# Appending the sample's new keys to the second half of the cached keys in a planned two-thread transformer step

## The chip, the core and the metric

One core of one Trainium2 chip runs one step of a four-branch encoder in float32. The metric is the device time of one execution, in microseconds, as the median of several. Busy times, waits and orders are read from one profiled execution and from the built programs.

## The reference, cut to what matters

Each of two layers projects the input, runs three parallel branches (a gated MLP, latent attention "B", stick-breaking attention "C"), mixes them and runs an MLP. It does so for a prompt of 512 rows and for a sample of 8 streams with 16 new rows each. In the sample, both attentions look at 1024 cached keys and at the stream's own 16 new ones:

```
ckv_all = jnp.concatenate([ckv_p, ckv], 1)     # 1024 cached + 16 new, per stream
k_all = jnp.concatenate([k_p, kc], 1)
...
scores = (einsum('bqhc,bkc->bhqk', q_lat, ckv) + einsum('bqhr,bkr->bhqk', q_rope, krope)) * MLA_SCALE
p = softmax(where(visible, scores, -inf)); out = einsum('bhqk,bkc->bqhc', p, ckv)
...
z = einsum('bqhd,bkhd->bhqk', q, k) * SB_SCALE
log_skip = where(mask, log_sigmoid(-z), 0); suffix = reversed cumsum(log_skip) - log_skip
w = where(mask, exp(log_sigmoid(z) + suffix), 0); out = einsum('bhqk,bkhd->bqhd', w, v)
```

## The kernel before, in words

The program consists of two threads, P (the prompt) and S (the sample). Each thread is a generator that records its instructions through the wrappers `Timed` (line 399; every compute instruction has line 417) and `Loads` (line 425; every DMA has line 433). `weave` alternates the threads while recording. Then `Plan.schedule` (line 209) takes the recorded instructions with their dependences and a table of costs (`cost_of`, line 379) and writes the order of every engine by list scheduling: for each engine it takes the ready instruction with the lowest rank. `ranks` spreads thread S over a fixed part of each layer of thread P. A buffer of a tag (a ring of `bufs` tiles) is granted in program order and comes free when the last instruction on it is placed. `follow` pins the order that results. All loads go through the one queue of SP.

A float32 number is split into a rounded high part and the remainder, `hi` and `lo` (`split`, line 611: ACT writes the high part, DVE or POOL the low one). Products are made of these parts.

Thread S runs, per layer, `s_prep`, then `lane_smla` (branch B, line 1545), then `lane_ssb` (branch C, line 1621), then its output projection and MLP (`s_out_mlp`). During the two lanes thread P runs its own latent attention, output projection and MLP on the tag `acc` of PSUM; S uses the tags `sC` (3 banks) and `x` (2 banks).

Both lanes go through four pairs of streams (`pr` 0 to 3; a stream in the pair is `j`). `pipeline` (line 1525) runs three steps on each pair:

- `front` calls `sample_scores` (line 1438). For each stream and each half `c` of its cache (512 keys) and each 128 of the key's 256 elements (`ct`), it loads 128x512 keys (`rawK`), splits them into the tile `cT` (POOL makes the low part), and multiplies (`block`): 64 rows of high and 64 rows of low queries stand side by side as the 128 columns of the stationary operand, so each product has 128 output rows. Branch B adds one product with the rotary keys `kr`. `fold_to` (line 1420) adds the low rows to the high rows: an ACT copy of 64 rows into `tmp`, a DVE addition into the row tile (`s2` in branch B, shown as `s`; `z` in branch C). The products of a half are accumulated in a bank of `sC` in branch B and of `x` in branch C.
- The new keys are a block of their own, `fresh` (line 1458): the 128 new keys of all eight streams (`cnT`/`krN`, `knTs`) are multiplied with the stream's queries into another bank of `sC`, folded into columns 1024 to 1151 of the row, and all but the pair's own are masked out by a window of a 224-column mask (`msk`). So a row has 1152 columns.
- `mid` makes the weights over the 1152 columns: a softmax, or the stick-breaking passes with a scan (`stick_weights`, line 701).
- `back` transposes the row in nine pieces of 128 columns (`weights_T`, line 1426, tile `pTs`), multiplies the first eight with the cached values (`cN`) and the ninth, of 128 new positions, with all 128 new values (`cnh`, `vn`; `fresh` in `sample_values`, line 1499), and folds the result.

`rms_to` (line 659) writes the squares that it only sums into one tile `junk` that both threads share.

Of the kernel before, what the change touches and what calls it, by code (L numbers as in the profile page):

```python
# [96 lines left out]
class Plan:  # L97
# [111 lines left out]
    def schedule(self, prio):  # L209
# [24 lines left out]
        for p, t in tags:  # L234
# [51 lines left out]
        def issue(k, e, s):  # L286
# [212 lines left out]
def hybrid_step(  # L499
# [156 lines left out]

    junk = cp.tile([128, 512], BF16, name="junk")
# [767 lines left out]

    def weights_T(pl, p):
        pTs = pl.tile([128, 9, 2, 2, 64], F32R, tag="pTs", name="pTs")
        for c0 in range(0, 9, 4):
            n = min(4, 9 - c0)
            yield at("sC", p)  # L1430
            pt = bank("sC")
            for i in range(n):
                tr(pt[:, i * 128:(i + 1) * 128], p[:, (c0 + i) * 128:(c0 + i + 1) * 128])
            split(pTs[:, c0:c0 + n, :, 0], pTs[:, c0:c0 + n, :, 1],
                  pt[:, :n * 128].rearrange("p (i j c) -> p i j c", j=2, c=64))
        return pTs

    def sample_scores(pl, s2, src, q_of, new, msk, n, kr_of=None, kr_new=None):

# [4 lines left out]
        def run(f):  # L1444
            return at("none" if f.args[3] else acc, *(x for x in f.args[4:] if x is not None))

        def block(j, q, c, ct, c4, kr):
            if ct == 0:
                held.append(bank(acc))
            s_ = held[0]  # L1450
            pe.matmul(s_, q[ct], c4[:, 0], start=(ct == 0), stop=False)
            pe.matmul(s_, q[ct], c4[:, 1], start=False, stop=(ct == 1 and kr is None))
            if ct:
                if kr is not None:
                    pe.matmul(s_, q[2], kr, start=False, stop=True)
                fold_to(s2[64 * j:64 * j + 64, 512 * c:512 * c + 512], held.pop(), 512, pl)

        def fresh(j, q, s_):
            for ct in range(2):
                pe.matmul(s_[:, :128], q[ct], new[:, 0, ct], start=(ct == 0), stop=False)  # L1460
                pe.matmul(s_[:, :128], q[ct], new[:, 1, ct], start=False, stop=(ct == 1 and kr_new is None))
            if kr_new is not None:
                pe.matmul(s_[:, :128], q[2], kr_new, start=False, stop=True)
            fold_to(s2[64 * j:64 * j + 64, 1024:], s_, 128, pl)

        for j in range(2):
            q = q_of(j)
            for c in range(2):
                kr = None
                for ct in range(2):  # L1470
                    raw = half(pl, "K", n)
                    ld.dma_start(raw, src(j, c)[:, ct])
                    c4 = pl.tile([128, 2, 512], F32R, tag="cT", name="cT", bufs=2)
                    split(c4[:, 0], c4[:, 1], raw, KLO)
# [12 lines left out]
    def sample_values(pl, pTs, src, new, done, n):  # L1487

# [56 lines left out]
    def lane_smla(l, ql):  # L1545
# [3 lines left out]
        olT = smp.tile([128, 2, NB, 4, QS], F32, name="olT")  # L1549
        msk = smp.tile([128, 224], F32, name="mskm")  # L1550
        ld.dma_start(msk, c_wide[:, 0])
# [8 lines left out]
        def front(pr):  # L1560
            s2 = st[pr] = smp.tile([128, 1152], F32, tag="s2", name="s2", bufs=2)

            def kr_of(j, c):
                raw = smp.tile([128, 512], F32, tag="krs", name="krs")
                ld.dma_start(raw, t_kr[l, 2 * pr + j, c])
                kr = smp.tile([128, 512], F32R, tag="kr", name="kr", bufs=2)
                act.copy(kr, raw)
                sub(kr[64:128], raw[64:128], kr[64:128], pool)
                return kr
# [3 lines left out]

            yield from sample_scores(smp, s2, keys(pr), q_of, cnT, msk[:, 96 - 32 * pr:224 - 32 * pr], KV["smla"][0], kr_of, krN)

# [6 lines left out]
        def back(pr, used):  # L1582
            s2, r = st.pop(pr)
            pTs = yield from weights_T(smp, s2)
            used[0] += 1
# [9 lines left out]

            yield from sample_values(smp, pTs, values(pr), cnh, done, KV["smla"][1])

# [23 lines left out]
    def lane_ssb(l):  # L1621
        sp_cm = pool_of(f"ssb{l}", "right")
        sp = sp_cm.__enter__()
        msk = sp.tile([128, 224], F32, name="msks")
        ld.dma_start(msk, c_wide[:, 1])
# [32 lines left out]
        def front(pr):  # L1658
            z = st[pr] = sp.tile([128, 1152], F32, tag="z", name="z", bufs=3)
# [4 lines left out]
            yield from sample_scores(sp, z, keys(pr), q_of, knT, msk[:, 96 - 32 * pr:224 - 32 * pr], KV["ssb"][0])  # L1664

        def mid(pr):
            z = st[pr]
            a = sp.tile([128, 1152], F32, tag="a", name="a")
            stick_weights(z, z, a, [(0, 1152)])

        def back(pr, used):
            pTs = yield from weights_T(sp, st.pop(pr))
            used[0] += 1
# [11 lines left out]

            yield from sample_values(sp, pTs, values(pr), vn, done, KV["ssb"][1])

# [125 lines left out]
def _constants():  # L1813
# [17 lines left out]

    x = np.arange(224)
    same = x[None, :] // QS == 6 + p[:, None] // 64
    wide = np.zeros((128, 2, 224), np.float32)
    wide[:, 0] = np.where(same, 0, neg)
# [66 lines left out]
```

## Time and profile before

| | |
|---|---|
| median of 3 runs | 1744.52 us (1735.86 to 1745.47) |
| the profiled execution's own time | 1738.5 us |
| its span, first to last instruction | 1736.6 us |
| PE busy | 1665.9 us (96%), 8756 matmuls |
| PE weight loads busy | 1404.2 us (81%) |
| DVE, ACT, POOL busy | 1167.8, 1017.5, 461.8 us |
| mean granted TensorE clock | 0.988 |

The profile's page gives busy time by engine, the same in 40 slices, the chain of work that ended last, and groups of equal instructions. "PE" is matmuls, "PEld" their weight loads, which run beside earlier matmuls. The busy time of a group counts the tails of its matmuls, which overlap the next ones; how far apart matmuls follow each other is read from the start times in the timeline, or from a long stretch of the chain.

### The profile page before, as it was taken

The numbers are of one execution on the slowest core, as the hardware profiler recorded it, in microseconds if no ns is written. First come the engines' busy times: TensorE is split into PE (matmuls) and PEld (weight loads), VectorE is DVE, ScalarE is ACT, GpSimd is POOL, SyncE is SP. The second block draws the span as 40 slices with busy tenths as digits, with TensorE's granted clock in tenths as the row PEclk, the third lists the DMA queues.
The fourth block names the chain that finished last, engine by engine and source line by source line (L and its number), as shares of the span: only waits on it lengthen the run. The fifth ranks groups of instructions, "written<-read, shape, count | busy, mean of one in ns | idle before, by whom it ended". The sixth has DMA issues, their size and how long they took to land.

```text
span 1736.6 us, 24320 instructions
## 1 busy us (share of the span) xinstructions
PE 1665.9 (96%) x8756; PEld 1404.2 (81%) x8756; DVE 1167.8 (67%) x1592; ACT 1017.5 (59%) x1891; POOL 461.8 (27%) x320
## 2 busy tenths in 40 slices
PE   8999999899998999999999989999999999999998
PEld 6898988787886778888878988888778778788886
DVE  3487776846675587666744876868467766776766
ACT  4586785546664556463335857855467656564632
POOL 0000446534664300000000004466446552000000
PEclk9999999999999999999999999999999999999999
DMA  7236565445444587674353255665465456875732
GB/s 260 92 97 184 184 186 197 157 151 186 158 153 133 182 274 251 204 246 141 130 165 105 91 170 171 197 217 170 142 184 168 134 154 232 265 246 191 252 125 84
DMA packets 145817, 305.05 MB, mean 176 GB/s; under 512 B 32032, under 2 KB 46496, under 8 KB 145696
## 3 DMA queue, kind: packets, MB, share of 16 engines
q1 hardware_dynamic: 145696, 303.49, 54.2%
q8 instruction: 69, 1.13, 0.3%
q14 instruction: 52, 0.43, 0.1%
HBM read 286.14 MB, written 17.30 MB: 175 GB/s over the span
## 4 chain that ended last, share of the span: by engine, by line
PE 73%; ACT 8%; DVE 7%; DMA 7%; issue 4%; POOL 2%; SPq 0%; ACTq 0%; POOLq 0%; DVEq 0%
PE acc L417 52%; PE sC L417 11%; PE x L417 10%; DVE xy L417 2%; POOL cN L417 1%; DMA rawV<-in_t_ckvv_dram 1%; DMA rawK<-in_t_sbk_dram 1%; ACT w L417 1%; POOL cT L417 1%; DVE w L417 1%; ACT cN L417 1%; ACT cT L417 1%; DMA rawS<-in_w_up_dram 1%; DVE a L417 1%; DMA rawP<-in_w_down_dram 0%
## 5 line engine op out<-in xcount | busy, mean ns | idle before, releaser
L417 PE MATMUL acc<-yT,wx 128*128 128x512 f32 (+1 forms) x1632 | 398.2, 385 | 3.9 <-DVE yT L417 3.8
L417 PE MATMUL acc<-w,hT 128*128 128x512 f32 x1536 | 395.1, 398 | 2.3 <-DVE hT L417 1.7
L417 PEld LDWEIGHTS acc<-yT,wx 128*128 128x128 f32 x1632 | 291.8, 191 | 61.4 <-issue 3.9
L417 PEld LDWEIGHTS acc<-w,hT 128*128 128x128 f32 x1536 | 283.1, 189 | 65.5 <-DVE hT L417 2.1
L417 POOL TENSOR_TENSOR cT<-rawK,cT 128x512 fp32r<-128x512 f32 x128 | 200.8, 1575 | 164.2 <-ACT cT L417 120.3
L417 POOL TENSOR_TENSOR cN<-rawV,cN 128x512 fp32r<-128x512 f32 x128 | 195.1, 1532 | 168.6 <-ACT cN L417 164.5
L417 DVE TENSOR_TENSOR wS<-rawS,wS 128x1024 fp32r<-128x1024 f32 x144 | 175.0, 1223 | 82.9 <-ACT wS L417 82.7
L417 DVE TENSOR_TENSOR w<-rawP,w 128x1024 fp32r<-128x1024 f32 (+4 forms) x122 | 149.0, 1227 | 111.6 <-ACT w L417 110.0
L417 ACT CAST wS<-rawS 128x1024 fp32r<-128x1024 f32 x144 | 150.8, 1051 | 117.8 <-PE x L417 66.4
L417 PE MATMUL acc<-w,xT 128*128 128x512 f32 (+3 forms) x960 | 190.1, 353 | 2.2 <-ACT w L417 1.1
L417 PEld LDWEIGHTS acc<-w,xT 128*128 128x128 f32 x960 | 159.8, 193 | 20.5 <-ACT w L417 1.5
L417 ACT CAST w<-rawP 128x1024 fp32r<-128x1024 f32 (+4 forms) x122 | 122.5, 1006 | 73.3 <-DMA rawP<-in_w_down_dram 36.4
L417 DVE TENSOR_TENSOR xy<-xy,acc 128x512 f32<-128x512 f32 x128 | 86.6, 683 | 71.4 <-PE acc L417 70.8
L417 ACT CAST cN<-rawV 128x512 fp32r<-128x512 f32 x128 | 78.5, 620 | 66.0 <-DMA rawV<-in_t_sbv_dram 30.1
L417 PE MATMUL x<-cN,pTs 128*128 128x256 f32 x512 | 92.4, 290 | 11.5 <-ACT cN L417 5.8
L417 PEld LDWEIGHTS x<-cN,pTs 128*128 128x128 f32 x512 | 77.7, 190 | 30.3 <-ACT cN L417 11.8
L417 ACT CAST cT<-rawK 128x512 fp32r<-128x512 f32 x128 | 79.2, 620 | 36.4 <-PE sC L417 14.4
L417 PE MATMUL x<-wS,htS 128*128 128x512 f32 x384 | 99.5, 393 | 0.8 <-ACT htS L417 0.8
L417 PE MATMUL sC<-wS,x1TS 128*128 128x512 f32 x384 | 98.4, 394 | 0.0
L417 DVE TENSOR_TENSOR wx<-rawP,wx 128x1024 fp32r<-128x1024 f32 x68 | 85.9, 1265 | 12.6 <-ACT wx L417 11.9
L417 PEld LDWEIGHTS x<-wS,htS 128*128 128x128 f32 x384 | 72.0, 188 | 17.7 <-ACT htS L417 1.2
L417 PEld LDWEIGHTS sC<-wS,x1TS 128*128 128x128 f32 x384 | 71.8, 188 | 16.5 <-DVE wS L417 0.5
(277 smaller groups left out, 2635.2 us busy)
## 6 DMA issues: line engine op xcount, KB each, us to landing
rawP<-in_t_wup_dram SPq DMA_DIRECT2D x64, 512.0 KB, 4.0
rawP<-in_w_down_dram SPq DMA_DIRECT2D x64, 512.0 KB, 4.2
rawS<-in_w_up_dram SPq DMA_DIRECT2D x64, 512.0 KB, 4.6
rawS<-in_w_down_dram SPq DMA_DIRECT2D x64, 512.0 KB, 4.3
rawK<-in_t_ckv_dram SPq DMA_DIRECT2D x64, 256.0 KB, 3.0
rawV<-in_t_ckvv_dram SPq DMA_DIRECT2D x64, 256.0 KB, 3.1
rawK<-in_t_sbk_dram SPq DMA_DIRECT2D x64, 256.0 KB, 3.1
rawV<-in_t_sbv_dram SPq DMA_DIRECT2D x64, 256.0 KB, 3.0
```

What stands on the lines that cost most here:

```text
L417: r = f(out, *a, **k)
```

## The change

In `sample_scores` the tiles of the second half of the cache become 544 columns wide. Their last 32 columns take the pair's 32 new keys by a small ACT copy from `cnT`, `knTs` or `krN`. The products of that half are done in two parts of 272 columns into two banks (in branch C the second bank comes from `sC`), each folded by itself, and the separate block of 128 new keys is gone. A row is 1056 columns, the mask 32. In `weights_T` the ninth piece has 32 columns; its transposed weights are put on the 32 partitions where the pair's new values stand, and the values' `fresh` multiplies 32 partitions instead of 128. The planner gets a rule: the first instructions on a buffer wait until the first instruction on the buffer before it in the ring has been placed. `junk` becomes one tile for each thread.

```diff
@@ Plan.schedule
+        begun = [set() for _ in range(n)]
+        for p, t in tags:
+            for a, b in zip(t["names"], t["names"][1:]):
+                mine = self.tiles[b]["ops"]
+                for k in mine:
+                    if not ops[k]["deps"] & mine:
+                        begun[min(self.tiles[a]["ops"])].add(k)
+        for ks in begun:
+            for k in ks:
+                need[k] += 1
...
+            for x in begun[k]:
+                ready[x] = max(ready[x], s)
+                need[x] -= 1
+                if not need[x] and x not in glued:
+                    loose(x)
@@ rms_to
-        act.activation(junk[:, :n], src, AF.Square, accum_out=ss)
+        act.activation(junk[now["by"]][:, :n], src, AF.Square, accum_out=ss)
@@ weights_T
-        for c0 in range(0, 9, 4):
+        for c0 in range(0, 8, 4):
...
+        tr(pt[:32, :128], p[:, 1024:])
+        k = slice(32 * pr, 32 * pr + 32)
+        split(pTs[k, 8, :, 0], pTs[k, 8, :, 1], pt[:32, :128].rearrange("p (j c) -> p j c", j=2))
@@ sample_scores
         def block(j, q, c, ct, c4, kr):
+            n = 272 if c else 512
             if ct == 0:
-                held.append(bank(acc))
-            s_ = held[0]
-            pe.matmul(s_, q[ct], c4[:, 0], start=(ct == 0), stop=False)
-            pe.matmul(s_, q[ct], c4[:, 1], start=False, stop=(ct == 1 and kr is None))
+                held.extend([bank(acc)] + ([bank("sC")] if c else []))
+            for e in range(2):
+                for i, s_ in enumerate(held):
+                    pe.matmul(s_[:, :n], q[ct], c4[:, e, i * n:i * n + n], start=(ct == 0 and e == 0), stop=(ct == e == 1 and kr is None))
...
-        def fresh(j, q, s_):
...
-            yield at("sC")
-            fresh(j, q, bank("sC"))
...
+                    c4 = pl.tile([128, 2, 544], F32R, tag="cT", name="cT", bufs=2)
+                    split(c4[:, 0, :512], c4[:, 1, :512], raw, KLO)
+                    if c:
+                        act.copy(c4[:, :, 512:], new[:, :, ct, 32 * pr:32 * pr + 32])
...
+                        if c:
+                            act.copy(kr[:, 512:], kr_new[:, 32 * pr:32 * pr + 32])
@@ sample_values
-            pe.matmul(po[:, :256], w[8], new[:, 0], start=False, stop=False)
-            pe.matmul(po[:, :256], w[8], new[:, 1], start=False, stop=True)
+            k = slice(32 * pr, 32 * pr + 32)
+            pe.matmul(po[:, :256], w[8][k], new[k, 0], start=False, stop=False)
+            pe.matmul(po[:, :256], w[8][k], new[k, 1], start=False, stop=True)
```

The planner writes a new order for every engine. Three places of it follow. In the rows of the changed kernel the wrapper's line is 433.

TensorE in branch B of layer 0, second pair of streams, where a stream's new keys are multiplied (`cT`, `cnT`, `kr`, `krN` are keys, `qlT` and `qrS` queries, rows on `acc` are thread P's). Before:

```order
L417 MATMUL acc<-knT,qT 128x256 x3
L417 MATMUL acc<-krT,qrT 128x256 x2
L417 MATMUL sC<-cnT,qlT 128x128 x4
L417 MATMUL sC<-krN,qrS 128x128
L417 MATMUL acc<-mask,identr 128x128
L417 MATMUL acc<-knT,qT 128x256 x2
L417 MATMUL sC<-cT,qlT 128x512 x2
```

Now:

```order
L433 MATMUL acc<-knT,qT 128x256 x3
L433 MATMUL acc<-krT,qrT 128x256
L433 MATMUL sC<-cT,qlT 128x272 x8
L433 MATMUL sC<-kr,qrS 128x272
L433 MATMUL acc<-krT,qrT 128x256
L433 MATMUL acc<-mask,identr 128x128
L433 MATMUL acc<-ckT,w_2663 128x256 x3
L433 MATMUL sC<-kr,qrS 128x272
```

The five products of 128 columns are gone; the half that had five of 512 columns has ten of 272, and P's products stand between them as before.

TensorE at the end of the values of a pair in branch B of layer 0 (`cnh` are the new values, `identr,o` and `identr,s` transposes). Before:

```order
L417 MATMUL x<-cN,pTs 128x256 x3
L417 MATMUL x<-cnh,pTs 128x256 x2
L417 MATMUL acc<-w_5537,hT 128x512 x2
L417 MATMUL acc<-w_5589,hT 128x512 x3
L417 MATMUL acc<-w_5352,hT 128x512 x2
L417 MATMUL sC<-identr,o 128x128 x2
L417 MATMUL sC<-identr,s_3039 128x128 x8
```

Now:

```order
L433 MATMUL x<-cnh,pTs 128x256 x2
L433 MATMUL acc<-w_5635,hT 128x512 x2
L433 MATMUL acc<-w_5720,hT 128x512 x3
L433 MATMUL acc<-w_5470,hT 128x512 x2
L433 MATMUL sC<-identr,o 128x128 x2
L433 MATMUL sC<-identr,s_3082 128x128 x8
L433 MATMUL acc<-w_5470,hT 128x512
L433 MATMUL sC<-identr,s_3082 32x128
L433 MATMUL acc<-w_5537,hT 128x512 x3
```

The two products on `cnh`, which now use 32 partitions, and the ninth transpose, which now has 32 output rows, stand alone between full-size products of thread P.

ACT in branch B of layer 0, second pair (`rawK` to `cT` is the high part of the keys). Before:

```order
L417 COPY tmp<-sC 64x512
L417 CAST cqT<-acc 128x3x128
L417 CAST ckT<-acc 128x512
L417 CAST cT<-rawK 128x512 x2
L417 CAST kr<-krs 128x512
```

Now:

```order
L433 CAST cT<-rawK 128x512
L433 CAST cqT<-acc 128x3x128
L433 CAST ckT<-acc 128x512
L433 COPY cT<-cnT 128x2x32
L433 COPY tmp<-sC 64x512
L433 CAST cT<-rawK 128x512
L433 COPY cT<-cnT 128x2x32
L433 CAST kr<-krs 128x512
```

The copies of the new keys stand behind the casts of the same tile.

## Rows read from the trace of the kernel before

**Rows 1.** The page: busy time of each engine, and granted clock in 40 slices.

```profile
PE 1665.9 (96%) x8756; PEld 1404.2 (81%) x8756; DVE 1167.8 (67%) x1592; ACT 1017.5 (59%) x1891; POOL 461.8 (27%) x320
...
PEclk9999999999999999999999999999999999999999
```

**Rows 2.** Busy time by stage: stretch, length, engines (instructions), clock, DMA share, GB/s.

```profile
20.00:210.00 190.00, 184.49 (x1218) 169.76 (x1217) 121.73 (x232) 125.15 (x308) 23.99 (x22) 0.99 0.46 145
210.00:600.00 390.00, 368.97 (x1936) 307.24 (x1935) 255.72 (x342) 236.99 (x440) 204.73 (x132) 0.98 0.52 163
...
868.00:1065.00 197.00, 185.81 (x1163) 168.35 (x1161) 122.82 (x226) 119.08 (x293) 12.57 (x14) 0.97 0.43 135
1065.00:1460.00 395.00, 380.05 (x2062) 317.61 (x2061) 274.16 (x367) 250.49 (x469) 216.13 (x140) 1.00 0.55 174
```

**Rows 3.** The chain that ended last, in time: start us, us, what; each layer's end.

```profile
821.14 46.55 PE acc L417 x200
...
1681.39 46.81 PE acc L417 x201
```

**Rows 4.** Timeline of PE, 40 to 60 us: start us, us, what; rows of equal width.

```profile
40.84 11.55 PE L417 MATMUL acc<-w,xT 128*128 128x256 f32 x96
52.23 0.60 PE L417 MATMUL sC<-identr,cc 128*128 128x128 f32 x4
52.59 5.86 PE L417 MATMUL acc<-w,xS 128*128 128x512 f32 x24
...
58.68 0.50 PE L417 MATMUL x<-kT,qP 128*128 128x128 f32 x3
...
59.02 0.28 PE L417 MATMUL x<-mask,identr 128*128 128x128 f32 x1
59.13 0.50 PE L417 MATMUL x<-kT,qP 128*128 128x128 f32 x3
```

**Rows 5.** Groups of PE by shape: count, busy us, mean ns, idle before.

```profile
L417 PE MATMUL acc<-w,hT 128*128 128x512 f32 x1536 | 395.1, 398 | 2.3 <-DVE hT L417 1.7 <-DVE xy L417 0.3 <-DVE w L417 0.2
...
L417 PE MATMUL sC<-cT,qlT 128*128 128x512 f32 x128 | 44.7, 415 | 1.2 <-POOL cT L417 0.8 <-ACT cT L417 0.2
...
L417 PE MATMUL sC<-cnT,qlT 128*128 128x128 f32 x64 | 9.7, 264 | 0.0
...
L417 PE MATMUL sC<-knTs,qS 128*128 128x128 f32 x64 | 9.4, 259 | 0.0
...
L417 PE MATMUL sC<-krN,qrS 128*128 128x128 f32 x16 | 4.4, 277 | 0.0
```

**Rows 6.** The weight loads of one of these groups.

```profile
L417 PEld LDWEIGHTS acc<-w,hT 128*128 128x128 f32 x1536 | 283.1, 189 | 65.5 <-DVE hT L417 2.1 <-DVE xy L417 0.8 <-DVE w L417 0.4
```

**Rows 7.** Groups of ACT: the folds, a pass over a row, two small copies.

```profile
L417 ACT COPY tmp<-sC 64x512 f32<-64x512 f32 x32 | 18.7, 584 | 5.8 <-PE sC L417 5.3
...
L417 ACT ACTIVATE a<-a 128x1152 f32<-128x1152 f32 x16 | 18.6, 1165 | 0.1
...
L417 ACT COPY tmp<-x 64x256 f32<-64x256 f32 x32 | 11.8, 369 | 35.3 <-PE x L417 34.6 <-DVE s L417 0.4
...
L417 ACT COPY tmp<-sC 64x128 f32<-64x128 f32 x32 | 8.4, 261 | 12.0 <-PE sC L417 4.3 <-DVE z L417 3.6 <-DVE s L417 3.3
...
L417 ACT COPY ycT<-sC 64x32 f32<-64x32 f32 x32 | 5.8, 181 | 4.2 <-PE sC L417 3.7
...
L417 ACT CAST kd<-ck 128x64 fp32r<-128x64 f32 x2 | 0.5, 236 | 1.2 <-DMA ck<-ckd 1.2
```

**Rows 8.** A group of POOL (page): the low part of the keys.

```profile
L417 POOL TENSOR_TENSOR cT<-rawK,cT 128x512 fp32r<-128x512 f32 x128 | 200.8, 1575 | 164.2 <-ACT cT L417 120.3
```

**Rows 9.** Waits of PE: who waited for whom, us in total, times, longest.

```profile
PE x L417 <- ACT cN L417: 5.8, 9, 1.6
PE x L417 <- POOL cN L417: 5.6, 3, 4.9
```

More of the change, by code (lines that the diff above doesn't have):

```diff
@@ L1424, in fold_to, with weights_T, sample_scores @@
         dve.tensor_tensor(out, pss[0:64, :n], tmp[:, :n], ALU.add)
-    def weights_T(pl, p):
+    def weights_T(pl, p, pr):
         pTs = pl.tile([128, 9, 2, 2, 64], F32R, tag="pTs", name="pTs")
-        for c0 in range(0, 9, 4):
-            n = min(4, 9 - c0)
+        for c0 in range(0, 8, 4):
             yield at("sC", p)
             pt = bank("sC")
-            for i in range(n):
+            for i in range(4):
                 tr(pt[:, i * 128:(i + 1) * 128], p[:, (c0 + i) * 128:(c0 + i + 1) * 128])
-            split(pTs[:, c0:c0 + n, :, 0], pTs[:, c0:c0 + n, :, 1],
-                  pt[:, :n * 128].rearrange("p (i j c) -> p i j c", j=2, c=64))
+            split(pTs[:, c0:c0 + 4, :, 0], pTs[:, c0:c0 + 4, :, 1], pt.rearrange("p (i j c) -> p i j c", j=2, c=64))
+        yield at("sC", p)
+        pt = bank("sC")
+        tr(pt[:32, :128], p[:, 1024:])
+        k = slice(32 * pr, 32 * pr + 32)
+        split(pTs[k, 8, :, 0], pTs[k, 8, :, 1], pt[:32, :128].rearrange("p (j c) -> p j c", j=2))
         return pTs
-    def sample_scores(pl, s2, src, q_of, new, msk, n, kr_of=None, kr_new=None):
+    def sample_scores(pl, s2, src, q_of, new, msk, n, pr, kr_of=None, kr_new=None):
         late, held = [], []
@@ L1444, in run @@
         def run(f):
-            return at("none" if f.args[3] else acc, *(x for x in f.args[4:] if x is not None))
+            return at("none" if f.args[3] else acc, *(x for x in f.args[4:6] if x is not None))
         def block(j, q, c, ct, c4, kr):
+            n = 272 if c else 512
             if ct == 0:
-                held.append(bank(acc))
-            s_ = held[0]
-            pe.matmul(s_, q[ct], c4[:, 0], start=(ct == 0), stop=False)
-            pe.matmul(s_, q[ct], c4[:, 1], start=False, stop=(ct == 1 and kr is None))
+                held.extend([bank(acc)] + ([bank("sC")] if c else []))
+            for e in range(2):
+                for i, s_ in enumerate(held):
+                    pe.matmul(s_[:, :n], q[ct], c4[:, e, i * n:i * n + n], start=(ct == 0 and e == 0), stop=(ct == e == 1 and kr is None))
             if ct:
-                if kr is not None:
-                    pe.matmul(s_, q[2], kr, start=False, stop=True)
-                fold_to(s2[64 * j:64 * j + 64, 512 * c:512 * c + 512], held.pop(), 512, pl)
-        def fresh(j, q, s_):
[L1459 to L1464, printed above, removed]
+                for i, s_ in enumerate(held):
+                    if kr is not None:
+                        pe.matmul(s_[:, :n], q[2], kr[:, i * n:i * n + n], start=False, stop=True)
+                    fold_to(s2[64 * j:64 * j + 64, 512 * c + i * n:512 * c + i * n + n], s_, n, pl)
+                held.clear()
         for j in range(2):
@@ L1485, in sample_scores, with sample_values @@
         dve.tensor_tensor(s2[:, 1024:], s2[:, 1024:], msk, ALU.add)
-    def sample_values(pl, pTs, src, new, done, n):
+    def sample_values(pl, pTs, src, new, done, n, pr):
         o = pl.tile([128, 256], F32, tag="o", name="o")
@@ L1565, in kr_of @@
                 ld.dma_start(raw, t_kr[l, 2 * pr + j, c])
-                kr = smp.tile([128, 512], F32R, tag="kr", name="kr", bufs=2)
-                act.copy(kr, raw)
-                sub(kr[64:128], raw[64:128], kr[64:128], pool)
+                kr = smp.tile([128, 544], F32R, tag="kr", name="kr", bufs=2)
+                act.copy(kr[:, :512], raw)
+                sub(kr[64:128, :512], raw[64:128], kr[64:128, :512], pool)
                 return kr
@@ L1583, in back @@
             s2, r = st.pop(pr)
-            pTs = yield from weights_T(smp, s2)
+            pTs = yield from weights_T(smp, s2, pr)
             used[0] += 1
@@ L1594, in done @@
                          pf[:, :256].rearrange("p (c x) -> p c x", c=2))
-            yield from sample_values(smp, pTs, values(pr), cnh, done, KV["smla"][1])
+            yield from sample_values(smp, pTs, values(pr), cnh, done, KV["smla"][1], pr)
         yield from pipeline(front, mid, back, 4)
@@ L1623, in lane_ssb @@
         sp = sp_cm.__enter__()
-        msk = sp.tile([128, 224], F32, name="msks")
+        msk = sp.tile([128, 32], F32, name="msks")
         ld.dma_start(msk, c_wide[:, 1])
@@ L1658, in front @@
         def front(pr):
-            z = st[pr] = sp.tile([128, 1152], F32, tag="z", name="z", bufs=3)
+            z = st[pr] = sp.tile([128, 1056], F32, tag="z", name="z", bufs=3)
             def q_of(j):
                 return [qS[:, ct, 2 * pr + j].rearrange("p a h q -> p (a h q)") for ct in range(2)]
-            yield from sample_scores(sp, z, keys(pr), q_of, knT, msk[:, 96 - 32 * pr:224 - 32 * pr], KV["ssb"][0])
+            yield from sample_scores(sp, z, keys(pr), q_of, knT, msk, KV["ssb"][0], pr)
         def mid(pr):
             z = st[pr]
-            a = sp.tile([128, 1152], F32, tag="a", name="a")
-            stick_weights(z, z, a, [(0, 1152)])
+            a = sp.tile([128, 1056], F32, tag="a", name="a")
+            stick_weights(z, z, a, [(0, 1056)])
         def back(pr, used):
-            pTs = yield from weights_T(sp, st.pop(pr))
+            pTs = yield from weights_T(sp, st.pop(pr), pr)
             used[0] += 1
@@ L1684, in done @@
                         act.copy(ycT[p_, ct, 32 * pr:32 * pr + 32].rearrange("p (j q) -> p j q", j=2), pv[p_, ct, :, 2 * ct + hf])
-            yield from sample_values(sp, pTs, values(pr), vn, done, KV["ssb"][1])
+            yield from sample_values(sp, pTs, values(pr), vn, done, KV["ssb"][1], pr)
         yield from pipeline(front, mid, back, 4, 3)
@@ L1830, in _constants @@
     mask[:, 1] = np.where(p[None, :] // 64 <= p[:, None] // 64, 0, neg)
-    x = np.arange(224)
-    same = x[None, :] // QS == 6 + p[:, None] // 64
-    wide = np.zeros((128, 2, 224), np.float32)
+    x = np.arange(32)
+    same = x[None, :] // QS == p[:, None] // 64
+    wide = np.zeros((128, 2, 32), np.float32)
     wide[:, 0] = np.where(same, 0, neg)
```

10 lines of the change are left out of this document (4 added, 6 removed).

## The prediction

> **What bounds the kernel now.** I read the page first: PE is busy for 1665.9 us of 1736.6 us, no other engine for more than 67%, and the granted clock stands at full level in nearly every slice [rows 1]. So PE is the candidate. A busy PE need not be the bound, therefore the stages come second. Thread S's two attention lanes lie in the stretches 210 to 600 us and 1065 to 1460 us. PE is busy for 368.97 of 390 us and 380.05 of 395 us there, while POOL, ACT and DVE each stay below 70% of the stretch [rows 2]. Thread P's products fill what S leaves free. Third, the chain that ended last: after S has finished its layer, P alone runs another 46.55 us (layer 0) and 46.81 us (layer 1) of products without a break [rows 3]. So S may finish up to 46 us later in a layer without moving the end, and a product fewer on PE, in either thread, lets P's work move up and the end come earlier. The currency is time on PE: its products, and the gaps between them.
>
> **What a product costs.** The mean of a row is no price, as it holds a tail that overlaps the next product: products of 512 columns read 398 ns [rows 5]. The price is the distance between starts. 200 products of 512 columns take 46.55 us [rows 3], 0.2328 us each. 96 products of 256 columns begin at 40.84 us and the next instruction at 52.23 us [rows 4]: 0.1186 us each. Four products of 128 columns begin at 58.68 us and the next four at 59.13 us [rows 4]: 0.1125 us each, hardly less than for 256 columns. 272 columns do not occur; on the line between 256 and 512 they cost 0.1186 + 16/256 x (0.2328 - 0.1186) = 0.1257 us. The bounds are 0.1186 and 0.2328 us; I take the line, since 256 is the near end.
>
> **The change, part by part.**
>
> *Scores, branch B.* For one stream, the second half of the cache had five products of 512 columns, and the new keys five of 128: 5 x 0.2328 + 5 x 0.1125 = 1.727 us. Now there are ten of 272: 1.257 us. Saved 0.470 us, for 8 streams in 2 layers 7.5 us.
>
> *Scores, branch C.* Four and four before, 1.381 us; eight now, 1.006 us. Saved 0.375 us, 16 times 6.0 us. Together **13.5 us** of PE. The products removed are the 64 + 64 + 16 of the new keys [rows 5]; the number of matmuls stays as it was, because the half that had one bank now has two.
>
> *The ninth transpose.* 16 in all, with 32 columns as weights instead of 128. Nothing in the trace has so few weight columns: the saving lies between nothing and their whole price, 16 x 0.1125 = 1.8 us. I take nothing, as the identity still streams 128 columns, and those cost 0.1125 us each in the rows.
>
> *The new values.* 64 products (two per stream, branch and layer) still stream 256 columns, but on 32 partitions instead of 128. Every matmul and weight load of the trace before uses the whole 128x128 array, so the price of changing over to a part of it and back is not in any row. The change makes 32 such pairs and 16 transposes, 48 places, each alone between full-size products, as the order shows: 96 changeovers. Below, the price is not nothing but a gain: if the pairs ran entirely beside their neighbours, 64 x 0.1186 = 7.6 us would go. Above, if each changeover let the array run empty and load weights in the open: the tail of a 512-column product, 0.398 - 0.233 = 0.165 us, and a weight load of 0.189 us [rows 5, 6], 0.354 us, 96 times 34 us. The nearest rows are four transposes between products of 256 and of 512 columns, from 52.23 to 52.59 us [rows 4]: PE changes over to another mode and back, and each still takes 0.09 us, less than a 128-column product. By them I take nothing, and keep 34 us as a rival.
> [...]
>
> *ACT.* Added are 64 copies of 128x64 elements, at 0.236 us by the cast of that size, and 16 of 128x32, at 0.181 us by the smallest copy [rows 7]: 18.0 us. The folds were 64 of 512 columns and 32 of 128 (45.7 us); now 32 of 512 and 64 of 272 at 0.369 + 16/256 x 0.215 = 0.382 us (43.1 us). The 40 passes over a row shrink by 96 of 1152 columns, at most 96/1152 of 1.165 us each [rows 7], 3.9 us. In sum ACT gains 12 us of work in 785 us of the lanes, where it is busy for 487 us [rows 2]. Cost on the path: nothing. A copy goes into the same tile as the low part of the keys, and POOL needs 1.575 us for that [rows 8], longer than the copy behind the cast. Without this cover each copy would add 0.24 us to a stream's block, 64 x 0.24 = 15 us over both layers, inside the 46 us that S may be late per layer.
>
> *DVE, POOL, DMA.* DVE loses some microseconds of folds, masks and passes, POOL does what it did, four masks get smaller. None of these is the bound, so nothing.
>
> *The order.* The planner's rule and the second dump tile remove no instruction and add none, but the order of all engines is computed anew. What a new order is worth is bounded by the trace itself: nearly the same work has 21.0 us of idle PE in the lanes of layer 0 and 15.0 in those of layer 1, and 5.5 and 11.2 us in the stretches ahead of them [rows 2]. So an order is worth about 6 us in a stretch, either way. I take nothing.
>
> **Sum.** The profiled execution took 1738.5 us, and 13.5 us less is 1725.0 us. That execution lies 6.0 us below the median of the runs, 1744.5 us, against which the changed kernel's median is to be held: **1731 us**, 0.8% faster.
>
> **The rivals.**
>
> *The changeovers eat the gain.* For it: 96 of them, and nothing beside them to hide behind, as PE is the bound. Against it: transposes cost the products around them nothing. With the smaller piece alone, the 0.165 us tail, 96 x 0.165 = 15.8 us: 1731 + 15.8 = 1746.8 us, no change that can be measured. [...]
>
> *The changeovers cost more than the gain.* Their place is the 48 spots above, their price up to 0.354 us. From (13.5 + 8.7) / 96 = 0.23 us per changeover the kernel is slower by 0.5%; at 0.354 us it takes 1731 + 34 = 1765 us. For it: weights are normally loaded beside an earlier product (PEld is busy for 81% of the span and PE waits little), and an array that must be empty first would lose that.
>
> *New waits in place of the products.* In branch B the second half holds two of the three banks of `sC` from its first product to its fold, and the transposes of the row and of the result want the same three banks; the products on `cT` also wait for one more copy. PE's waits for S are few today, 5.8 and 5.6 us for the values `cN` [rows 9]. For it: the stretches differ by 6 us already; two such stretches for the worse in each layer make 24 us, half of that undoes the gain: about 1731 + 13 = 1744 us, the same; with all of it 1755 us, slower. Against it: P has products to put into any gap, and the order lists them between S's as before.
>
> *The change does not do what it says.* The order rules it out: the products of 128 columns are gone, those of 272 are there.
>
> **How the numbers follow.** The forecast, 1731 us, has 0.50. The changeovers at the tail's price, 1747 us, have 0.17; at a higher price, 1765 us, 0.08. New waits have 0.25, of which 0.05 with a slower kernel. A measurement of this kernel can tell about 0.5%, 8.7 us, from no change. So faster by over 0.5%: 0.50; within 0.5%: 0.17 + 0.20 = 0.37; slower: 0.13. The forecast's own range is 1722 to 1737 us: down by the 7.6 and 1.8 us that the new values and the ninth transposes could still give, up by the 6 us of an order. The range for 8 in 10 reaches up over both cases of no change, 1748 us, and leaves out the slower ones; down it goes to 1718 us, as one run of before lay 9 us below its median.
>
> **What the profile of the changed kernel would show.** Right: groups of 272 columns with starts 0.126 us apart; PE busy some 13 us less; idle PE in the lanes' stretches near 21 and 15 us; P's lone ends still some 46 us long. Wrong by changeovers: gaps of 0.1 us or more around the products on `cnh` and `vn` and around the transposes with 32 output rows. Wrong by waits: PE waiting for `sC` banks (ACT `tmp`, DVE `pTs`) or for `cT`. The prediction falls if PE is busy 13 us less and the span is not shorter, or if the lone end of P shrinks to nothing.

## The result, and the profile after

The changed kernel took 1751.25 us (median of 12 runs, 1747.49 to 1755.44) against 1739.36 us for the kernel before in the same comparison (12 runs, 1733.86 to 1746.18). The ratio is **1.0061, interval 1.0046 to 1.0077**: slower by 0.6%, some 11 us. The prediction, 1731 us and faster, was wrong, and the time lies above its range (1718 to 1748 us). The profiled execution took 1748.7 us with a span of 1746.6 us, 10.0 us more than before.

The page of the changed kernel, against [rows 1]:

```profile
PE 1673.0 (96%) x8756; PEld 1409.6 (81%) x8756; DVE 1159.1 (66%) x1592; ACT 1022.8 (59%) x1971; POOL 444.3 (25%) x320
...
PEclk9999999899999999999999999998999999999999
```

PE is busy for 7.1 us more, although its products stream fewer columns. Two slices show a lower granted clock than any slice of before. The other engines moved by under 18 us and stay far from the bound.

The same stretches as in [rows 2] (stretch, length, busy us of PE, PEld, DVE, ACT, POOL with instructions, clock, DMA share, GB/s):

```profile
20.00:210.00 190.00, 180.32 (x1177) 166.54 (x1176) 115.51 (x225) 120.94 (x304) 21.47 (x21) 0.98 0.43 138
210.00:600.00 390.00, 372.36 (x1969) 310.50 (x1968) 259.40 (x348) 242.67 (x481) 194.92 (x134) 0.98 0.53 165
868.00:1065.00 197.00, 187.06 (x1170) 169.64 (x1169) 124.03 (x228) 119.90 (x296) 13.25 (x14) 0.97 0.44 135
1065.00:1460.00 395.00, 375.44 (x2009) 312.62 (x2008) 261.01 (x358) 247.21 (x491) 210.25 (x140) 0.97 0.53 166
```

The idle time of PE grew in two stretches: ahead of the lanes of layer 0 (9.7 us, before 5.5), where the change edits nothing but the order, and in the lanes of layer 1 (19.6 us, before 15.0), where the clock fell from 1.00 to 0.97 of full. In the other two it shrank, to 17.6 and 9.9 us (before 21.0 and 11.2).

The chain's last pieces of the two layers, as in [rows 3]:

```profile
822.53 46.59 PE acc L433 x200
...
1691.75 46.79 PE acc L433 x201
```

P's lone ends are as long as before, so the currency of the prediction held: whatever time PE gains or loses earlier moves the end. The last one begins 10.4 us later than before.

**Where 10 us come from.** I took the start times of all 8756 matmuls of an execution and set each distance to the next against a price by its columns, all read in the traces: 0.232 us for 512 columns, 0.174 for 384, 0.147 for 320, 0.126 for 272, 0.119 for 256, 0.110 for 128, 0.111 for 64. What a distance is longer than its price went to one heading: beside a product on 32 partitions; under half the granted clock (0.50 of full, for example from 323.9 to 334.1 us in the changed kernel); otherwise a wait, by its size. The ends ahead of the first and behind the last matmul, 16 us, are the same in all.

| us, one execution each | products at their price | beside products on 32 partitions | waits of 0.5 us and more | smaller waits | half clock | span |
|---|---|---|---|---|---|---|
| before | 1623.8 | 0 | 57.0 | 29.0 | 10.5 | 1736.6 |
| after | 1610.9 | 8.9 | 62.1 | 31.9 | 17.0 | 1746.6 |
| e1_tile_only | 1623.8 | 9.2 | 58.4 | 27.9 | 9.0 | 1744.7 |
| e3_rule_only | 1623.8 | 0 | 68.2 | 29.8 | 14.8 | 1752.5 |
| e4_no_rule | 1610.9 | 9.1 | 55.1 | 32.4 | 9.9 | 1732.9 |
| e9_same_order_full_values | 1610.9 | 0 | 60.7 | 34.8 | 16.6 | 1738.8 |
| e10_no_rule_full_values | 1610.9 | 0 | 61.4 | 34.5 | 12.3 | 1734.8 |
| e6_own_ring | 1610.9 | 0 | 60.8 | 30.2 | 10.9 | 1727.8 |

The shorter products are there, 12.9 us. Against them stand 8.9 us beside the products on 32 partitions, 8.0 us of waits and 6.5 us of half clock. The columns of the products and of the pairs are alike wherever the products and the tile are alike. Waits and clock vary by several us between executions of one order too (e4 and e10: 55.1 and 61.4 us of long waits), so for them the medians below decide. How much goes to the half clock also depends on the price that is taken there: by the distances that the traces show at the half clock, 0.427 us for 512 columns and 0.213 us for 256 and for 128, it is 13.4 us before and 20.6 us after, and the waits are some 3 us less in both.

**The new values.** The end of a pair's values, first in the kernel before (timeline of PE and of its weight loads, rows of the other engines left out; start us, us, what):

```profile
451.44 0.52 PE L417 MATMUL x<-cN,pTs 128*128 128x256 f32 x3
451.68 0.31 PEld L417 LDWEIGHTS x<-vn,pTs 128*128 128x128 f32 x2
451.80 0.40 PE L417 MATMUL x<-vn,pTs 128*128 128x256 f32 x2
451.92 0.54 PEld L417 LDWEIGHTS acc<-yT,wx 128*128 128x128 f32 x3
452.04 0.86 PE L417 MATMUL acc<-yT,wx 128*128 128x512 f32 x3
```

and the same place in the changed one:

```profile
458.14 0.51 PE L433 MATMUL x<-cN,pTs 128*128 128x256 f32 x3
458.58 0.29 PEld L433 LDWEIGHTS x<-vn,pTs 32*128 32x128 f32 x2
458.58 0.50 PE L433 MATMUL x<-vn,pTs 32*128 32x256 f32 x2
...
459.01 0.53 PEld L433 LDWEIGHTS acc<-yT,wx 128*128 128x128 f32 x3
459.01 0.73 PE L433 MATMUL acc<-yT,wx 128*128 128x512 f32 x2
```

Before, three products and then two follow each other 0.12 us apart, and each load of weights begins 0.12 us ahead of its product, beside the earlier one. Now the first load on 32 partitions and its product have one start, and so have the next full-size load and its product: in all 32 pairs of this trace these two loads begin at most 0.002 us ahead. The three take 0.44 us, 0.084 more than their price, and the two 0.43 us, 0.193 more than theirs: **0.28 us for a pair**, 32 pairs, 8.9 us. Why the loads at the two ends of a pair no longer run ahead is not shown. The two products of a pair, on the same 32 partitions, are apart as well (0.22 us), but there the load does run ahead: two loads of 0.18 us take 0.29 us together, so the second begins 0.11 us behind the first product and 0.12 us ahead of its own product. Before, it begins with the first product, at most 0.004 us behind it in 31 of the 32 pairs. I read this gap as part of the first change; no run shows the two apart.

The groups (by shape; count, busy us, mean ns, idle before) answer to [rows 5] and [rows 6]:

```profile
L433 PE MATMUL sC<-cT,qlT 128*128 128x272 f32 x128 | 24.4, 300 | 0.2
...
L433 PE MATMUL x<-vn,pTs 32*128 32x256 f32 x32 | 8.3, 339 | 0.0
...
L433 PE MATMUL x<-cnh,pTs 32*128 32x256 f32 x32 | 8.0, 328 | 0.0
...
L433 PEld LDWEIGHTS x<-vn,pTs 32*128 32x128 f32 x32 | 4.9, 190 | 2.5 <-issue 0.6
```

The idle column of PE shows 0.0 for these products: the lost time lies inside their neighbours' and their own busy time, and shows only in the start times and in the idle time ahead of the weight loads.

The ninth transpose, with 32 columns as weights, among full-size products (timeline of PE, after):

```profile
358.00 0.94 PE L433 MATMUL acc<-yT,wx 128*128 128x512 f32 x3
358.78 0.27 PE L433 MATMUL sC<-identr,s 128*32 128x128 f32 x1
358.81 1.42 PE L433 MATMUL acc<-w,hT 128*128 128x512 f32 x5
```

The next product begins 0.03 us behind it, where a transpose of 128 columns holds it off for 0.11 us. So it is in 13 of the 16; the other three distances are 0.33 to 0.69 us.

**The waits.** PE's waits for DVE (who for whom; us in all, times, longest), after:

```profile
PE acc L433 <- DVE xy L433: 12.2, 8, 5.4
...
PE acc L433 <- DVE ev L433: 6.5, 3, 2.8
```

against before:

```profile
PE acc L417 <- DVE yT L417: 4.7, 3, 3.8
PE acc L417 <- DVE xy L417: 4.5, 4, 3.2
```

The wait for `ev` is new; it comes with the planner's rule (e3, e4). The wait for `xy`, thread P's rows, is 10.0 to 12.2 us in all seven kernels with the shorter products and 3.8 to 7.8 us in the five without. Part of that is a change of name: the wait for `yT`, the next tile of the same chain of P on DVE, falls from 4.7 us before to 0.5 us after. The two together are 11.1 to 13.3 us in the seven and 8.9 to 10.3 us in the five, so 1 to 4 us more. As I read it, this chain is late next, and fewer of S's products stand in its gap. The longest pieces of the wait in the changed kernel (timeline of PE):

```profile
326.07 1.09 PE L433 MATMUL acc<-identr,xy 128*128 128x128 f32 x4 [4.43 <-DVE xy L433]
...
1194.61 1.09 PE L433 MATMUL acc<-identr,xy 128*128 128x128 f32 x4 [5.38 <-DVE xy L433]
```

In the kernel before these two products waited 0.60 and 3.16 us, but just ahead of the first PE had waited for the same chain:

```profile
323.17 0.77 PE L417 MATMUL acc<-yT,wx 128*128 128x256 f32 x2 [3.76 <-DVE yT L417]
```

So it is the second place that grew. The stretch around it, after:

```profile
1180.00:1200.00 20.00, 12.83 (x70) 10.78 (x69) 18.79 (x20) 9.92 (x23) 14.72 (x8) 0.77 0.27 82
```

and before:

```profile
1180.00:1200.00 20.00, 16.74 (x102) 14.73 (x101) 18.40 (x20) 10.11 (x19) 17.27 (x9) 0.91 0.44 143
```

DVE is busy for 18.8 of the 20 us, and was for 18.4 before: it is the late one in both, and PE has 70 products in the stretch instead of 102. Beside the wait stands the clock: from 1.7 us into the wait of 5.38 us it is granted at 0.50 of full, from 1190.9 to 1201.1 us, and before from 1192.6 to 1196.0 us only (0.77 of full in the mean of this stretch, 0.91 before).

### The profile page after: what moved, and what is told of

It is laid out like the page before. It is cut to its first block, busy times and chain, and to the rows that moved or that the text cites. A ratio compares the mean times of both kernels' runs of the same rounds, so it can differ in the third digit from the quotient of the medians.

```text
span 1746.6 us, 24405 instructions
## 1 busy us (share of the span) xinstructions
PE 1673.0 (96%) x8756; PEld 1409.6 (81%) x8756; DVE 1159.1 (66%) x1592; ACT 1022.8 (59%) x1971; POOL 444.3 (25%) x320
## 4 chain that ended last, share of the span: by engine, by line
PE 72%; ACT 7%; DVE 7%; DMA 6%; issue 5%; POOL 3%; SPq 0%; POOLq 0%; ACTq 0%; DVEq 0%
PE acc L433 52%; PE sC L433 10%; PE x L433 9%; POOL cT L433 2%; DMA rawK<-in_t_sbk_dram 2%; DMA rawV<-in_t_ckvv_dram 1%; DVE xy L433 1%; POOL cN L433 1%; DVE w L433 1%; ACT cT L433 1%; ACT w L433 1%; DMA rawP<-in_w_down_dram 1%; DVE wx L433 1%; DMA rawS<-in_w_up_dram 1%; ACT cN L433 0%
## 5 line engine op out<-in xcount | busy, mean ns | idle before, releaser
L433 PE MATMUL acc<-w,hT 128*128 128x512 f32 x1536 | 399.4, 400 | 4.5 <-ACT hT L433 3.5
L433 PEld LDWEIGHTS acc<-yT,wx 128*128 128x128 f32 x1632 | 293.6, 193 | 60.7 <-DVE wx L433 2.9
L433 POOL TENSOR_TENSOR cT<-rawK,cT 128x512 fp32r<-128x512 f32 x128 | 194.2, 1522 | 196.9 <-ACT cT L433 168.9
L433 POOL TENSOR_TENSOR cN<-rawV,cN 128x512 fp32r<-128x512 f32 x128 | 186.2, 1462 | 180.2 <-ACT cN L433 168.4
L433 ACT CAST w<-rawP 128x1024 fp32r<-128x1024 f32 (+4 forms) x122 | 122.0, 1003 | 74.2 <-DMA rawP<-in_w_down_dram 34.8
L433 DVE TENSOR_TENSOR wx<-rawP,wx 128x1024 fp32r<-128x1024 f32 x68 | 93.1, 1372 | 18.8 <-ACT wx L433 18.1
L433 ACT CAST cT<-rawK 128x512 fp32r<-128x512 f32 x128 | 79.3, 621 | 44.5 <-DMA rawK<-in_t_sbk_dram 17.6
```

The costliest lines, as they stand in the source:

```text
L433: r = f(out, *a, **k)
```

## The experiments

Theory A: the two products on 32 partitions cost time. Theory B: the order that the planner's rule makes costs time. Rival C: the shorter products themselves bring nothing. All ratios are to the kernel before on the same chip, from five rounds, with their 95% intervals.

**e1_tile_only**: the kernel before, with only the tile of the new values changed; every engine's order is that of before.

```diff
-            pe.matmul(po[:, :256], w[8], new[:, 0], start=False, stop=False)
-            pe.matmul(po[:, :256], w[8], new[:, 1], start=False, stop=True)
+            k = slice(32 * pr, 32 * pr + 32)
+            pe.matmul(po[:, :256], w[8][k], new[k, 0], start=False, stop=False)
+            pe.matmul(po[:, :256], w[8][k], new[k, 1], start=False, stop=True)
```

What it no longer multiplies are the other pairs' rows, whose weights are zero.

> The kernel before, in which only the two products of each stream on the new values use the pair's 32 partitions instead of all 128 (the weights of the others are zero, so the result is the same). The order of every engine stays as it was. If products on a part of the array cost the changed kernel its 8.9 us, as its trace reads, this kernel is 8 to 10 us slower than before, ratio about 1.005, and the pair's two starts are 0.22 us apart instead of 0.12. If the slowdown is the new order's alone, the ratio is 1.000.

Measured: 1746.61 us, ratio 1.0028 [1.0006, 1.0050]. Its timeline at the place shown above:

```profile
456.42 0.51 PE L417 MATMUL x<-cN,pTs 128*128 128x256 f32 x3
456.87 0.29 PEld L417 LDWEIGHTS x<-vn,pTs 32*128 32x128 f32 x2
456.87 0.50 PE L417 MATMUL x<-vn,pTs 32*128 32x256 f32 x2
...
457.29 0.30 PEld L417 LDWEIGHTS acc<-yT,wx 128*128 128x128 f32 x2
457.29 0.50 PE L417 MATMUL acc<-yT,wx 128*128 128x512 f32 x1
```

0.45 and 0.42 us where before has 0.36 and 0.24: 0.27 us more, in an order that is otherwise that of before. The trace shows 9.2 us for the 32 pairs, the medians about 5 (interval 1 to 9 us). That part of the loss falls where PE would have waited anyway would explain the difference, but is not shown.

**e2_full_values**: the changed kernel with the new values on 128 partitions, the other pairs' weights set to zero by a planned instruction.

```diff
+        pool.memset(r32(pTs[:, 8]), 0.0)
...
-            k = slice(32 * pr, 32 * pr + 32)
-            pe.matmul(po[:, :256], w[8][k], new[k, 0], start=False, stop=False)
-            pe.matmul(po[:, :256], w[8][k], new[k, 1], start=False, stop=True)
+            pe.matmul(po[:, :256], w[8], new[:, 0], start=False, stop=False)
+            pe.matmul(po[:, :256], w[8], new[:, 1], start=False, stop=True)
```

> The changed kernel with the new values' products on all 128 partitions again: the other 96 partitions of the transposed weights are set to zero by POOL, 16 times. If the part of the array costs 9 us, this is 8 to 10 us faster than the changed kernel, about 1.001 of before. If it costs nothing, it stays at 1.006 of before. The order moves a little, so 3 us either way belong to that.

Measured: 1736.02 us, 0.9963 [0.9943, 0.9982]. The kernel is now faster than before, so A gains and C loses (e10 tells more on C). But the 0.98% between this and the changed kernel, 17 us, are more than the pairs' 9: the added instruction moves the order as well, so e2 alone doesn't price the pairs (e9 does).

**e3_rule_only**: the kernel before with the planner's rule (the `Plan.schedule` part of the diff above) and nothing else.

> The kernel before with only the planner's rule added: no instruction more or less, a new order. If the rule makes an order with more waits and with more stretches at the half clock, this is 8 to 15 us slower than before (ratio 1.005 to 1.009). If the rule only lets the plan through and the part of the array and the wider keys do the rest, the ratio lies within 0.997 and 1.003.

Measured: 1750.81 us, 1.0053 [1.0031, 1.0075]. The rule alone costs about 9 us, with the old products, the old tile and one `junk` for both threads.

**e4_no_rule**: the changed kernel without the rule.

```diff
-        begun = [set() for _ in range(n)]
...
-            for x in begun[k]:
-                ready[x] = max(ready[x], s)
-                need[x] -= 1
-                if not need[x] and x not in glued:
-                    loose(x)
```

> The changed kernel without the planner's rule. If the rule costs the time, this is 8 to 15 us faster than the changed kernel, about 1.000 of before. If the order with the wider keys is bad with or without the rule, it stays within 4 us of the changed kernel, 1.004 to 1.008 of before.

Measured: 1739.24 us, 0.9987 [0.9964, 1.0010]. Without the rule the change is level with before. From 0.9987 to 1.0061, some 13 us, the rule decides.

In the plan of before the rule is broken by four instructions only, two per layer, all on the scratch ring `gt` of the gated MLP (two buffers, `wsn`, `tmp` and `ya` in turn): the load of the prompt's gating weights `wsn`, placed ahead of the sample's product `ya` on DVE, and ACT's squares of the prompt's second group into `tmp`, placed ahead of the first group's `ya`. The next two runs bind one kind each.

**e7_load_tie**: e3 with the rule for loads alone. **e8_squares_tie**: for ACT alone (`"act"` in place of `"sp"`).

```diff
-                    if not ops[k]["deps"] & mine:
+                    if ops[k]["eng"] == "sp" and not ops[k]["deps"] & mine:
```

> The kernel before with only those ties of the rule that bind a load: one per layer that matters, the load of the prompt's gating weights behind the sample group's product in the ring gt. The orders of PE, POOL and SP stay as before; ACT and DVE move some ten instructions. Ratio 0.998 to 1.002 if the order of PE carries the cost; about 1.005 if it is the late gating weights.

> The kernel before with only those ties of the rule that bind an ACT instruction: one per layer that matters, the squares of the second prompt group behind the product of the first in the ring gt. The orders of PE, POOL and SP become those of e3_rule_only. Ratio 1.004 to 1.009 if this one tie carries the rule's cost; within 0.998 to 1.002 if not.

Measured: e7 1740.16 us, 0.9997 [0.9978, 1.0016]; e8 1754.20 us, 1.0082 [1.0057, 1.0108]. The tie of the squares carries the whole cost. PE's waits in e3:

```profile
PE acc L433 <- DVE ev L433: 7.1, 3, 2.8
```

and in e8:

```profile
PE acc L433 <- DVE ev L433: 6.7, 3, 2.9
```

The waits for `ev` are absent before, in e7 and in e4. At one place (timeline of PE in the gated MLP of layer 0), the changed kernel:

```profile
135.59 2.50 PE L433 MATMUL acc<-w,xT 128*128 128x320 f32 x16
140.93 0.72 PE L433 MATMUL acc<-w,xT 128*128 128x320 f32 x3 [2.83 <-DVE ev L433]
```

and e4:

```profile
135.68 2.50 PE L417 MATMUL acc<-w,xT 128*128 128x320 f32 x16
139.63 0.33 PE L417 MATMUL sC<-gh,wsT 128*128 128x128 f32 x1 [1.45 <-ACT gh L417]
```

The tie shows on DVE. Without it (before) the sum of the second group's squares, `gst`, stands between the two instructions on the first group's `ya` (shown as `gt`, like all tiles of the ring):

```profile
133.90 0.68 DVE L417 TENSOR_TENSOR gt<-sC,bsc 128x512 f32<-128x512 f32 x1
134.50 0.67 DVE L417 TENSOR_REDUCE gst<-gt 128x8 f32<-128x512 f32 x1
135.09 0.68 DVE L417 TENSOR_TENSOR gt<-gt,xy 128x512 f32<-128x512 f32 x1
```

With it (changed kernel) it stands behind both:

```profile
134.40 0.69 DVE L433 TENSOR_TENSOR gt<-sC,bsc 128x512 f32<-128x512 f32 x1
...
135.47 0.69 DVE L433 TENSOR_TENSOR gt<-gt,xy 128x512 f32<-128x512 f32 x1
136.07 0.68 DVE L433 TENSOR_REDUCE gst<-gt 128x8 f32<-128x512 f32 x1
```

The second group's `gh` begins on ACT at 140.84 us instead of 138.03, TensorE's order has P's products ahead of those on `gh`, and they wait for a bank that DVE evicts (`ev`) at 140.26 us. It is not evicted later than before (140.89 us): there TensorE waited at the same place for `gh` (1.16 us) and `cqT` (0.62 us). So the waits for `ev`, 7 us in e3, in part replace others, and the loss is clearer a little later. PE from 150 to 190 us, before and in e3 (as in [rows 2]):

```profile
150.00:190.00 40.00, 38.44 (x301) 36.69 (x300) 27.79 (x67) 26.06 (x66) 8.09 (x8) 1.00 0.57 175
150.00:190.00 40.00, 34.77 (x243) 33.91 (x241) 21.54 (x57) 19.52 (x50) 2.38 (x3) 0.87 0.39 118
```

e3 waits 3.4 us for `krT` (ACT) there and runs for 10 us at the half clock. e4 is as before (301 products, clock 1.00), the changed kernel lies between (265, 0.91). By the distances of starts, 9 of the 16 us that the profiled execution of e3 lost are lost ahead of the lanes of layer 0.

**e5_best**: e2 with the rule for every ring but `gt` (first diff). **e6_own_ring**: e2 with the whole rule, but `wsn` on a ring of its own (second).

```diff
+            if t["names"] and t["names"][0].startswith("gt_"):
+                continue
```

```diff
-        wsn = pl.tile([128, 512], F32, tag="gt", name="gt", bufs=2).rearrange("p (g c) -> p g c", g=4)
+        wsn = pl.tile([128, 512], F32, tag="wsn", name="wsn").rearrange("p (g c) -> p g c", g=4)
```

> The changed kernel with both suspected costs out: the new values on all 128 partitions again (as in e2_full_values), and the planner's rule for every ring but the gMLP's scratch ring gt, the only one in which it moves anything. If the two costs are what the change lost (about 9 us for the part of the array, about 10 us for the rule) and the shorter products keep their 13 us, this is 12 to 18 us faster than the changed kernel's 1751 against a before of 1741, that is a ratio of 0.990 to 0.995, and faster than e2_full_values. If the rule's order was no cost of its own, it stays at 0.996.

> e2_full_values, the planner's rule whole, but the gMLP's gating weights get a ring of their own instead of two tiles of gt, so that the rule no longer ties their load to the gMLP's scratch. It keeps the other tie, the second prompt group's squares behind the first group's product. If the load's tie is the costly one, about 0.991; if the squares' tie is, about 0.996 as e2_full_values.

Measured: e5 1733.45 us, 0.9956 [0.9939, 0.9973]; e6 **1730.53 us, 0.9941 [0.9924, 0.9957]**, the fastest of all, 10 us below before. Neither shows a wait for `ev`. e5 gained hardly more than e2 (0.07%, give or take some 0.26), which has the rule on `gt` too and waits 6.6 us for `ev`: in e2's order the tie costs little. e6 keeps the tie of the squares and its wait for `krT` (1.8 us), and is the fastest. So the waits for `ev` and `krT` are marks of the tie, but not shown to be the whole way in which it costs; that stays open. e6 also gives the gated MLP one buffer more than any other kernel here; the kernel before with that buffer was not run, so its 0.59% is not the change's alone.

**e9_same_order_full_values**: the changed kernel with the values on 128 partitions as in e2, the zeros written ahead of the plan, so that TensorE, ACT, DVE and SP keep the changed kernel's order. **e10_no_rule_full_values**: the same edit to e4. The diff shows the line of the zeros; the products are changed as in e2.

```diff
+        nc.gpsimd.memset(r32(pTs[:, 8]), 0.0)
```

> The changed kernel with the new values on all 128 partitions, as e2_full_values, but with the 16 POOL writes of zeros left out of the plan, so that PE, ACT, DVE and SP keep the changed kernel's order instruction by instruction. The trace gives the 32 pairs 8.9 us. If PE's delays add up in the end, this is 9 us faster than the changed kernel (ratio to before 1.001); if other waits take up about half of them, as e1_tile_only says, 5 us (1.003). If e2_full_values gained its 15 us mostly by its new order, this stays above 1.000.

> The order of e4_no_rule (no planner's rule) with the new values on all 128 partitions, zeros again outside the plan. Only the shorter products on the keys are left of the change. Expected 5 to 9 us below e4_no_rule, ratio 0.993 to 0.996, the same as e5_best and e6_own_ring within 3 us; 0.9925 if the 13 us of shorter products came through whole.

Measured: e9 1741.06 us, 1.0000 [0.9981, 1.0019]; e10 1736.74 us, 0.9963 [0.9941, 0.9985]. In the changed kernel's own order the pairs are worth 0.61%, 10.6 us; without the rule 0.24%, 4 us (e4 to e10); in the order of before 0.28%, 5 us (e1). With the pairs gone the rule still takes 0.37%, 6.5 us (e10 to e9), with them 13 us (e4 to the changed kernel). Each of these differences is uncertain by 4 to 6 us. So the pairs' cost is clear of noise in two of the three orders and the rule's in e3, e8 and with or without the pairs; whether the two simply add, or the order decides how much of the pairs' 9 us reaches the end, is not shown. In e10 only the shorter products, a second `junk` and the order that comes of them are left, and it is faster than before by 0.37% [0.15, 0.59]: C falls. A second `junk` alone was not tried.

The rest of the order's part can be read from the plan. `Plan.schedule` works out an end of its own order (`self.span`, an estimate by the costs of `cost_of`, no measurement). It is 1678.5 us for the kernel before and e1, 1678.4 for e7, 1688.9 and 1689.0 for e3 and e8, 1682.4 for the changed kernel and e9, 1676.8 for e4 and e10, and 1670.7, 1665.3 and 1663.7 for e2, e5 and e6. The kernels without pairs on 32 partitions stand in the same sequence by this end and by their measured ratios, in which only e2 and e10, and before and e9, are level. By it the tie of the squares costs 10.5 us in the order of before, and e2's order is 11.7 us shorter than the changed kernel's, which is most of the 17 us between them. The price of the pairs is not in it, since `cost_of` goes by columns alone.

## Why the prediction was wrong

- **The shorter products: right.** 13.5 us were forecast, 12.9 us came; a product of 272 columns takes 0.125 us (0.1257 forecast): eight begin at 454.75 us and the next instruction at 455.75 us. What reaches the end is less: e10, e5 and e6, which have neither the pairs on 32 partitions nor the waits for `ev`, gain 0.37 to 0.59%, 6 to 10 us, each in an order of its own. P's chain on DVE (`xy`, `yT`) is late next and takes back 1 to 4 us; the prediction set DVE at nothing and named no such wait.
- **The new values, "By them I take nothing": wrong, the first step that failed.** They cost 8.9 us on TensorE. I took the four transposes of full size between products as the nearest rows; they use the whole array, and so said nothing on a part of it; that PE runs them in another mode is in no row. The rival of the changeovers came nearest, for the loads at the two ends of a pair do begin with their products (at most 0.002 us ahead), but its place and price were others: not 96 changeovers but 32 pairs of 0.28 us, 0.08 to 0.09 on either side and 0.10 within. No run shows an array that runs empty, nor the tail of 0.165 us as its price. The 16 transposes with 32 columns cost nothing: behind 13 of them the next product begins 0.08 us sooner than behind one of 128 columns. With the distances ahead of them, and without the longer ones that I take for waits, they gave back some 0.7 us of the 1.8 us that the prediction named as the most.
- **The order, "I take nothing": wrong, the second step.** The rule alone costs 9 us, and by e4 some 13 us of the changed kernel's time. Idle PE in the four stretches moved by 1.3 to 4.6 us, within the bound of 6 us, but an order also moves the half clock, which is no idle time: 10.5 us before, 14.8 us in e3, 17.0 us after, one execution each. The costly tie lies in the gated MLP, where the prediction looked at no row of the order. Nor did it ask the plan: its end came 3.9 us later than before, although by the planner's costs the products are nearly 13 us less.
- **Right**: P's lone ends, 46.6 and 46.8 us, and no S on the path there; POOL and DVE off the bound as engines; ACT's 80 new copies of 0.21 to 0.25 us without a wait of their own among PE's large ones.
- **The sum.** 13 us gained, 9 us lost to the pairs, and 8 and 6.5 us to waits and half clock. The lower end of the range, 1718 us, does not follow from the reason given for it: 1731 less 9 is 1722. "PE busy some 13 us less" was no good sign to look for: busy time holds tails, half clock and the gaps beside the pairs, and rose by 7 us.
- **The rivals.** "New waits in place of the products" came true in kind, at and behind the gated MLP and at P's `xy`, not at the `sC` banks. The rival on the other side wanted 0.23 us per changeover; per pair on 32 partitions 0.28 us were paid, but at a third as many places, and it took the order besides to make the kernel slower.

## What to carry to other kernels

A smaller contraction was no cheaper product here: between full-size products, two on 32 of 128 partitions took 0.28 us more than two on all 128, and with zeros on the unused partitions (e9) the ratio went from 1.0061 to 1.0000. A planner's rule is a change of its own: list which instructions of the old order it forbids, look at the stage where they stand, compare the end that the planner itself works out with and without it, and time the rule alone before it is mixed with an edit that saves work. Where PE is the bound, price by distances of starts, and expect that the next engine's chain takes back a part of what is saved (here DVE's, 1 to 4 us).

## What the runs showed of the hardware that I had not expected

- At the change from full-size products to products on 32 partitions, and back, the load of the weights begins with its product (at most 0.002 us ahead, all 32 pairs); before, at the same place, it runs 0.12 us ahead, beside the earlier product. Within the pair it runs 0.12 us ahead as well, and the second product follows the first after 0.22 us instead of 0.12 us. The 64 loads on 32 partitions take as long as those on 128 (183 to 190 ns against 189, [rows 6]).
- Loading 32 of the array's columns, with all 128 rows (the ninth transposes), shows no such price among full-size products: the next product begins 0.03 us later, against 0.11 us behind a full transpose.
- From 2.3 and 1.7 us into the waits of 4.43 and 5.38 us the granted clock was 0.50 of full for 10.2 us each time (323.9 to 334.1 us and 1190.9 to 1201.1 us; 0.74 in the mean from 320 to 340 us, 0.77 from 1180 to 1200 us). Behind the wait of 2.83 us for `ev` it stayed at 1.00 (138 to 150 us). In the profiled executions half-clock stretches make 63 us after and 44 us before, and lengthened the work by 17.0 and 10.5 us by the table, 20.6 and 13.4 by the distances at the half clock, time that comes on top of the waits. That a wait brings the half clock is my reading; no run shows it.
